# All turns of a two-layer decoder by DMA transposes, with every engine's order laid out by the kernel itself

## The chip, the cores and the metric

The kernel runs on one core of a Trainium2 chip. The core has a matrix engine (PE; PEld is its loading of weights), a vector engine (DVE), a scalar engine (ACT), a general engine (POOL) and an engine that issues transfers (SP); sixteen DMA engines carry the transfers. Each engine works through its own list of instructions in order and waits on semaphores for the others. The metric is the time of one execution on the device, in microseconds (us); lower is better.

## The reference

Two layers over 256 positions of width 1024. In each layer one input projection makes eight groups of 512 columns, two mixers of four heads each use them, an output projection adds to the residual stream, and a gated embedding is added after it:

```python
for i in range(DEPTH):                                 # DEPTH = 2
    h = rms_norm(x, norm_g[i])
    proj = h @ w_in[i]                                 # 1024 x 4096
    rq, rk, rv, rz, mq, mk, mv, mz = jnp.split(proj, cuts, axis=-1)
    r_out = retention(rotary(heads(rq)), rotary(heads(rk)), heads(rv), ret_norm_g[i])
    r_out = jax.nn.silu(rz) * r_out
    m_out = moba(rms_norm(heads(mq), q_norm_g[i]), rms_norm(heads(mk), k_norm_g[i]), heads(mv), rel_bias)
    m_out = jax.nn.silu(mz) * m_out
    x = x + jnp.concatenate([r_out, m_out], -1) @ w_out[i]
    gate = jax.nn.sigmoid(rms_norm(x) @ w_ple_gate[i])
    x = x + gate * rms_norm(p[i] @ w_ple[i], ple_norm_g[i])
```

At this length `moba` is plain causal softmax attention with a bias by distance, and `retention` is causal attention with a fixed decay in place of the softmax, followed by a norm per head.

## The kernel before

Every large product is made in three matmuls. Both factors are split into a high and a low part, and the kernel adds high by high, high by low and low by high (`mm3`, lines 143 to 148). I call these three matmuls a triple: they take one block of 128 inputs for one half `m` of the 256 positions to 512 outputs. A stage of weights (1 MB, `stage`, line 122) is loaded into one of four buffers `wst`, and `load_w` (lines 129 to 141) splits each half of it: ACT casts the high part `wh`, DVE subtracts it to get the low part `wl`. Six such pairs of parts exist. Each pair feeds 4 triples.

In a layer PE goes through the groups MQ, MK, RQ, RK, MZ, MV, RV, RZ (16 triples each), then the output projection (32 triples, `acc` banks filled first from the moba half, then from the retention half, line 612 and line 630), then the gate (32 triples, line 668). The attention matmuls are put in between: `moba_scores` (line 474), `moba_out` (510), `ret_scores` (525), `ret_out` (539).

What a matmul reads as its left factor has to lie with its inputs along the partitions, so results have to be turned. The kernel does it in two ways.

* By DMA: `halves` (line 252) lets ACT copy a 128x512 block of 4-byte values into two planes of 16-bit halves `u`; `turned_by_dma` (258) issues one DMA transpose of both planes into `w`, and two DVE copies put the halves together again (line 265). The heads of MQ, MK, RQ, RK and both mixers' outputs go this way: 12 blocks a layer.
* By PE: `transposed` (line 248) multiplies four 128x128 blocks with an identity (line 250) into a PSUM bank. ACT copies it out (line 497), or ACT and DVE split it into high and low parts (`evac_parts`, lines 283 and 284). The softmax probabilities (`turn`, 493: three blocks a layer) and the residual stream (`turn_x`, 625: four blocks of `x1T` in each layer, and four of the next layer's input `aT` after layer 0) go this way: 18 blocks of four matmuls.

The order on PE and SP is the order in which the code is written (`manual_schedule`, line 59): work behind a result is put off by a number of ticks (`later` and `tick`, lines 82 to 94), weight loads are called ahead when buffers come free. The instructions of ACT, DVE and POOL are laid by the framework's own scheduler, by priorities (`PRIO`).

Of the kernel before, what the change touches and what calls it, by code (L numbers as in the profile page):

```python
# [11 lines left out]
F32 = mybir.dt.float32  # L12
# [6 lines left out]
P = 128  # L19
# [18 lines left out]
PRIO = 300  # L38
AHEAD = 3
LATE = 5  # L40
# [12 lines left out]


@with_exitstack
def tile_hybrid_trunk(ctx: ExitStack, tc: tile.TileContext, first, rest, x, pT, ple_g, rel_bias,
                      w_in, w_out, w_ple, w_gate, consts, out):
    nc = tc.nc
    ctx.enter_context(tc.manual_schedule(engines={mybir.EngineType.PE, mybir.EngineType.SP}))
# [4 lines left out]

    cp = pool("cp", 1)
# [5 lines left out]
    big = pool("big", 2)  # L71
    tmp_p = pool("tmp", 4)
    tok_p = pool("tok", 3)
    sm = pool("sm", 4)
# [4 lines left out]
    pending = []  # L79
    now = [0]  # L80

    def later(delay, fn, prio=PRIO):

        pending.append((now[0] + delay, fn, prio))

    def tick():
        now[0] += 1
        tick_now()

    def tick_now():  # L90
        due = [e for e in pending if e[0] <= now[0]]
        pending[:] = [e for e in pending if e[0] > now[0]]
        for _, f, prio in due:
            with tc.high_priority(offset=prio):
                f()

    jobs, got = [], {}

    def job(key, fn):
        jobs.append((key, fn))  # L100

    def fetch(key):

        while key not in got:
            load_next()
        used.add(key)
        return got[key]

    def load_next():
        k, fn = jobs.pop(0)  # L110
        r = fn()
        if k is not None:
            got[k] = r

    def ahead():

        while jobs and len(got) - len(used) <= AHEAD:
            load_next()

    used = set()  # L120

    def stage(key, src):
        def fn():
            st = wst_p.tile([P, 4, GW], F32, name="wst")
            nc.sync.dma_start(st, src)
            return st
        job(key, fn)

    def load_w(key):

        st = fetch(key)
        parts = []
        for c in range(2):
            hi = wh_p.tile([P, 2, GW], F32R, name="wh")
            lo = wl_p.tile([P, 2, GW], F32R, name="wl")
            s = st[:, 2 * c:2 * c + 2]
            nc.scalar.copy(hi, s)  # L137
            nc.vector.tensor_tensor(lo, s, hi.bitcast(F32), op=ALU.subtract)  # L138
            parts.append((hi, lo))
        ahead()  # L140
        return parts

    def mm3(ps, a, k, w, kk, start, stop):
        ah, al = a
        wh, wl = w
        nc.tensor.matmul(ps, ah[:, k], wh[:, kk], start=start, stop=False)  # L146
        nc.tensor.matmul(ps, ah[:, k], wl[:, kk], start=False, stop=False)  # L147
        nc.tensor.matmul(ps, al[:, k], wh[:, kk], start=False, stop=stop)  # L148

    def act_tiles():  # L150
        both = act_p.tile([P, KT, 2, S], F32R, name="a")
        hi, lo = both[:, :, 0], both[:, :, 1]
        return [(hi[:, :, m * P:(m + 1) * P], lo[:, :, m * P:(m + 1) * P]) for m in range(MT)], hi, lo, both

    def rsqrt(dst, src, scale):
        n = src.shape[-1]
        t = sm.tile([P, 8], F32, name="rs_t")
        nc.vector.tensor_scalar(t[:, :n], src, scale, EPS, op0=ALU.mult, op1=ALU.add)  # L158
        nc.gpsimd.tensor_tensor(dst, t[:, :n], neghalf[:, :n], op=ALU.pow)  # L159

    par = cp.tile([P, Q_END], F32, name="par")
    warm = sm.tile([P, 1], F32, name="warm")
# [5 lines left out]
    for i in range(WARM):  # L168
        nc.tensor.matmul(ps0, idle[:, :P], idle, start=True, stop=True)
    x_t = xp.tile([P, MT, D], F32, name="x_t")  # L170
# [7 lines left out]
    bt = tmp_p.tile([P, GW], F32, name="tmp")[:H, :SPAN]  # L178
# [5 lines left out]
    def bias_table():  # L184
# [8 lines left out]
        d = dram.tile([H, SPAN], F32, name="bd")  # L193
        job(None, lambda: nc.sync.dma_start(d, bt))
        return bass.AP(tensor=d.tensor, offset=d.offset, ap=[[1, P], [SPAN, H], [1, S]])

    tbias = cp.tile([P, H, S], F32, name="tb")

    a0, a0h, a0l, a0b = act_tiles()

    def first_blocks(half):


        def fn():
            got = []
            for c in range(2):
                if half:
                    t = wst_p.tile([P, 4, GW], F32, name="wst").rearrange("p k n -> p (k n)")
                else:
                    t = xp.tile([P, MT, D], F32, name="E", bufs=2).rearrange("p m n -> p (m n)")  # L210
                at = 0
                for j in range(2):
                    k = half * 4 + 2 * c + j
# [551 lines left out]
```

## Time and profile before

| | us |
|---|---|
| median of 3 runs | 314.04 (314.0 to 314.89) |
| the profiled execution's own time | 314.63 |
| its span | 312.5 |
| PE busy | 307.1 (98%) |
| DVE busy | 241.4 (77%) |
| ACT busy | 190.6 (61%) |
| POOL busy | 27.4 (9%) |

The times of the parts below are read from the profiled execution. Its span begins with the first instruction and ends with the last; 2.1 us of its time lie around the span. A matmul's duration in the profile is longer than the distance to the next, since matmuls are pipelined; the distance is what counts for a sum.

### The profile page before, as it was taken

To read this page: it belongs to the slowest core of one execution; us is meant where nothing else is said; L and a number is where in the kernel's file an instruction comes from. 1 tells how busy PE (TensorE), PEld (TensorE's weight loads), DVE (VectorE), ACT (ScalarE), POOL (GpSimd) and SP (SyncE) were. 2 spreads that over 40 slices of the span, in tenths; PEclk is the share of its full clock that TensorE was granted. 3 is DMA by queue.
4 is the path that set the end of the run, shared out by engine and by line. 5 is a ranking of instruction groups with operands and counts; after the bars stand their busy time and mean duration, and the time that the engine had idled before them with its cause. 6 is when DMAs were issued, how large, how long until landed. Compare 5 with 4: busy or idle time off the path is not lost.

```text
span 312.5 us, 4188 instructions
## 1 busy us (share of the span) xinstructions
PE 307.1 (98%) x1465; PEld 255.8 (82%) x1465; DVE 241.4 (77%) x434; ACT 190.6 (61%) x330; POOL 27.4 (9%) x45
## 2 busy tenths in 40 slices
PE   8999999999999999999999999999999999999994
PEld 4888888888888888888888888888888888888884
DVE  4798899875599986949698877989747798959632
ACT  5887973866553746845485988447736536557411
POOL 4015100000002000101001521000000012000000
PEclk9999999999999999999999999999999999999998
DMA  7999949659791099200997569750496950770001
GB/s 266 419 412 415 273 90 401 115 122 382 274 348 55 6 262 421 87 0 24 379 397 271 198 127 297 303 160 0 115 367 258 289 181 2 176 294 2 34 35 67
DMA packets 35844, 65.03 MB, mean 208 GB/s; under 512 B 26476, under 2 KB 27248, under 8 KB 29680
## 3 DMA queue, kind: packets, MB, share of 16 engines
q1 hardware_dynamic: 35816, 64.78, 61.0%
q8 instruction: 11, 0.18, 0.2%
q14 instruction: 9, 0.07, 0.1%
q10 hardware_dynamic: 8, 0.00, 0.0%
HBM read 57.42 MB, written 1.05 MB: 187 GB/s over the span
## 4 chain that ended last, share of the span: by engine, by line
PE 97%; DMA 1%; DVE 1%; ACT 0%; issue 0%
PE acc L147 28%; PE acc L148 28%; PE acc L146 28%; PE mix L506 3%; PE mix L250 3%; PE mix L482 2%; PE mix L146 1%; PE mix L147 1%; PE mix L148 1%; DMA E<-in_first 1%; PE mix L528 1%; PE mix L529 1%; DVE wl L243 0%; DVE a L241 0%; ACT tmp L660 0%; DVE tmp L661 0%
## 5 line engine op out<-in xcount | busy, mean ns | idle before, releaser
L146 PE MATMUL acc<-wh,a 128*128 128x512 f32 (+1 forms) x392 | 153.3, 391 | 0.0
L147 PE MATMUL acc<-wl,a 128*128 128x512 f32 (+1 forms) x392 | 151.3, 386 | 0.1
L148 PE MATMUL acc<-wh,a 128*128 128x512 f32 (+1 forms) x392 | 151.2, 386 | 0.0
L137 ACT CAST wh<-wst 128x1024 fp32r<-128x1024 f32 x96 | 99.2, 1055 | 55.1 <-PE acc L148 33.7
L138 DVE TENSOR_TENSOR wl<-wst,wh 128x1024 fp32r<-128x1024 f32 x96 | 115.7, 1218 | 16.1 <-ACT wh L137 15.7
L146 PEld LDWEIGHTS acc<-wh,a 128*128 128x128 f32 x392 | 73.9, 189 | 14.7 <-ACT wh L236 0.6
L148 PEld LDWEIGHTS acc<-wh,a 128*128 128x128 f32 x392 | 73.8, 188 | 14.9
L147 PEld LDWEIGHTS acc<-wl,a 128*128 128x128 f32 x392 | 73.8, 188 | 14.7 <-DVE wl L243 0.6
L255 ACT COPY u<-tok 128x1024 uint16<-128x1024 uint16 x24 | 25.2, 1056 | 7.8 <-DVE tok L518 5.5
L265 DVE COPY T<-w 128x512 uint16<-128x512 uint16 x32 | 12.9, 454 | 8.9 <-DMA w<-u 8.9
L660 ACT ACTIVATE tmp<-acc,hr 128x512 f32<-128x512 f32 (+1 forms) x9 | 5.8, 640 | 19.4 <-PE acc L148 17.7
L159 POOL TENSOR_TENSOR ro<-rs_t,neghalf 128x4 f32<-128x4 f32 x4 | 4.9, 1234 | 134.9 <-DVE rs_t L158 134.9
L661 DVE SCALAR_TENSOR_TENSOR tmp<-tmp,E 128x512 f32<-128x512 f32 (+1 forms) x9 | 5.7, 631 | 13.7 <-ACT tmp L660 13.7
L283 ACT CAST a<-tmp 128x512 fp32r<-128x512 f32 x12 | 7.4, 618 | 10.4 <-DVE tmp L280 5.7
L506 PEld LDWEIGHTS mix<-V,PS 128*128 128x128 f32 x96 | 11.3, 192 | 0.3
L265 DVE COPY tmp<-w 128x512 uint16<-128x512 uint16 x16 | 6.4, 454 | 6.7 <-DMA w<-u 6.6
L506 PE MATMUL mix<-V,PS 128*128 128x128 f32 x96 | 11.4, 275 | 0.0
L434 POOL TENSOR_TENSOR qr<-qms,neghalf 128x4 f32<-128x4 f32 x8 | 10.0, 1263 | 13.5 <-DVE qms L432 10.5
L429 ACT ACTIVATE tmp<-acc 128x128 f32<-128x128 f32 x32 | 8.4, 289 | 1.4 <-PE acc L148 1.4
L284 DVE TENSOR_TENSOR a<-tmp,a 128x512 fp32r<-128x512 f32 x12 | 8.2, 682 | 0.7 <-ACT a L283 0.7
L283 ACT CAST a<-mix 128x512 fp32r<-128x512 f32 x8 | 4.7, 583 | 5.7 <-PE mix L250 5.6
L469 ACT ACTIVATE tmp<-acc,hr 128x512 f32<-128x512 f32 x8 | 5.5, 701 | 3.8 <-PE acc L148 3.8
(96 smaller groups left out, 255.9 us busy)
## 6 DMA issues: line engine op xcount, KB each, us to landing
wst<-in_w_in SPq DMA_DIRECT2D x30, 1024.0 KB, 7.6
wst<-in_w_out SPq DMA_DIRECT2D x8, 1024.0 KB, 5.0
wst<-in_w_gate SPq DMA_DIRECT2D x8, 1024.0 KB, 8.6
wst<-in_w_ple SPq DMA_DIRECT2D x2, 1024.0 KB, 6.0
wst<-in_rest SPq DMA_DIRECT2D x4, 384.0 KB, 6.6
E<-in_rest SPq DMA_DIRECT2D x3, 384.0 KB, 4.9
x_t<-in_x SPq DMA_DIRECT2D x2, 512.0 KB, 11.3
gb<-in_ple_g SPq DMA_DIRECT2D x2, 512.0 KB, 5.9
```

The costliest lines, as they stand in the source:

```text
L137: nc.scalar.copy(hi, s)
L138: nc.vector.tensor_tensor(lo, s, hi.bitcast(F32), op=ALU.subtract)
L146: nc.tensor.matmul(ps, ah[:, k], wh[:, kk], start=start, stop=False)
L147: nc.tensor.matmul(ps, ah[:, k], wl[:, kk], start=False, stop=False)
L148: nc.tensor.matmul(ps, al[:, k], wh[:, kk], start=False, stop=stop)
L250: nc.tensor.transpose(ps[:, j * P:(j + 1) * P], src[:, b * P:(b + 1) * P], ident)
L255: nc.scalar.copy(u, src.bitcast(U16).rearrange("p (n t) -> p t n", t=2))
L265: nc.vector.tensor_copy(raw[:, t], w[:, t])
L283: nc.scalar.copy(h, src)
L429: nc.scalar.activation(junk[:, sl], ps[m][:, sl], AF.Square, accum_out=ss[:, h:h + 1])
L434: nc.gpsimd.tensor_tensor(r, t, neghalf[:, :H], op=ALU.pow)
L506: nc.tensor.matmul(ps[:, h * DH:(h + 1) * DH], lhs(h, m, b), v[:, b, h * DH:(h + 1) * DH], start=b == 0, stop=b == m)
```

## The change

The identity and all 72 matmuls with it are gone. Probabilities and residual stream are turned as the heads already were: `halves` on ACT, one DMA transpose, two copies on DVE, and for the residual stream the split into high and low parts from the buffer in SBUF.

The ticks, the queue of load jobs and the priorities are replaced by a planner. `Flow` keeps a clock for each engine and one for the DMA engines. Each piece of work is a generator that names, step by step, its engine, an estimated duration and what it needs (`ask`); the planner takes the step that could start first, and among those that could start by then the one with the smallest key (a due time on PE's clock), and the step's instruction is written then. So the order of ACT, DVE, POOL and SP is fixed in the program too.

The order of PE changes in four places. Layer 0's moba scores stand after 58 triples instead of 64. Layer 1 projects MQ and MK together, by halves of the positions. `embed` (24 matmuls of the embedding) stands whole between the output projection and the gate in each layer, instead of in pieces around the gate. And the turns are gone.

The core of the diff:

```diff
-    ident = cp.tile([P, P], F32, name="ident")
-    make_identity(nc, ident)
...
-    ctx.enter_context(tc.manual_schedule(engines={mybir.EngineType.PE, mybir.EngineType.SP}))
+    ctx.enter_context(tc.manual_schedule(engines={E_.PE, E_.SP, E_.Activation, E_.DVE, E_.Pool}))
...
+class Flow:
...
+    def pick(self):
+        best = None
+        by = {}
+        for c in self.live:
+            r = self.can(c)
+            if r is not None:
+                by.setdefault(c.want[0], []).append((r, c))
+        for eng, cs in by.items():
+            start = max(self.clock[eng], min(r for r, _ in cs))
+            if best is None or start < best[0]:
+                best = start, eng, cs
+        if best is None:
+            return None
+        start, eng, cs = best
+        return start, min((c for r, c in cs if r <= start), key=lambda c: c.key() if callable(c.key) else c.key)
+
+    def lay(self, start, c):
+        eng, cost, take, after, mb = c.want
...
+        self.end = self.clock[eng] = start + cost
+        c.ready, c.on = self.end, eng
+        if mb is not None:
+            self.dma = max(self.dma, start + 1.3) + (2.7 * mb if mb else 0.8)
+            c.ready = self.dma + 0.9
...
-    def transposed(src, blocks, ps):
-        for j, b in enumerate(blocks):
-            nc.tensor.transpose(ps[:, j * P:(j + 1) * P], src[:, b * P:(b + 1) * P], ident)
-
-    def halves(src):
-
-        u = tok_p.tile([P, 2, GW], U16, name="u16", bufs=3)
+    def halves(src, name):
+
+        yield ask(ACT, 0.95, take=("u16",))
+        u = tok_p.tile([P, 2, GW], U16, name="u16", bufs=U_BUFS)
         nc.scalar.copy(u, src.bitcast(U16).rearrange("p (n t) -> p t n", t=2))
...
+    def turned(u, raw, take=()):
+
+
+        yield ask(SP, 1.25, take=("w16",), mb=TURN)
+        w = tok_p.tile([P, 2, 4, P], U16, name="w16", bufs=W_BUFS)
+        nc.sync.dma_start(w.rearrange("p t h k -> p (t h) k"), u.rearrange("p t n -> p (t n)"),
+                          transpose=True)
+        yield ask(DVE, 0.35, take=take)
...
+            nc.vector.tensor_copy(v, w[:, t].rearrange("p (h b) k -> p h (b k)", h=v.shape[1]))
...
-            def turn():
-
-                pt = mix_p.tile([P, 512], F32, name="mix")
-                transposed(s, range(4), pt)
-                nc.scalar.copy(PT[:, h0:h0 + per, m * P:m * P + n], pt.rearrange("p (h t) -> p h t", h=per))
-            later(7, turn)
...
+            u = yield from halves(s, "tok")
+            raw = box["PT"].bitcast(U16).rearrange("p h (k t) -> p t h k", t=2)
+            yield from turned(u, lambda: raw[:, :, h0:h0 + per, m * P:m * P + n])
...
-        def turn_x(dst, m, n, gains=None):
-            pt = mix_p.tile([P, 512], F32, name="mix")
-            transposed(x_t[:, m, n * GW:(n + 1) * GW], range(4), pt)
-            evac_parts(dst[m], n * 4, pt, 4, gains)
...
+        def added(m, n, ps):
+            xs = x_t[:, m, n * GW:(n + 1) * GW]
+            yield ask(DVE, 0.605)
+            nc.vector.tensor_tensor(xs, ps, xs, op=ALU.add)
+            flow.free("acc")
+            u = yield from halves(xs, None)
+            sq.append(flow.begin(squares([xs], SQ[m][:, n:n + 1]), flow.soon(3), flow.end))
+            yield from to_parts(x1T, m, n * 4, u)
...
+        groups.append(([both(TC, MQ, MK), lambda: [L_B]], moba_scores, 3, 2.5))
+        groups.append(([lambda: [PC.get(k) for k in ((0, 0), (1, 0), (1, 2))], both(VC, MV), both(TC, RQ, RK)],
+                       moba_out, 2, 2.0))
```

How the instructions stand at three places. First PE in layer 0, in the last triples of the output projection for the first half of the positions, before (L250 is the turn, `mix` its PSUM bank, `x_t` the residual stream):

```order
L146 MATMUL acc_1106<-wh_1214,a_140 128x512
L147 MATMUL acc_1106<-wl_1215,a_140 128x512
L148 MATMUL acc_1106<-wh_1214,a_140 128x512
L250 MATMUL mix_1247<-ident_115,x_t_111 128x128 x4
L146 MATMUL acc_1107<-wh_1200,a_140 128x512
L147 MATMUL acc_1107<-wl_1201,a_140 128x512
L148 MATMUL acc_1107<-wh_1200,a_140 128x512
```

And PE at the end of the same projection, now (L580 and L581 are the first of the 24 matmuls of `embed`):

```order
L314 MATMUL acc_1177<-wh_1171,a_125 128x512
L315 MATMUL acc_1177<-wl_1172,a_125 128x512
L316 MATMUL acc_1177<-wh_1171,a_125 128x512
L580 MATMUL mix_1299<-wh_1193,ph_392 128x512
L581 MATMUL mix_1299<-wl_1194,ph_392 128x512
```

No turn stands between the triples any more, and `embed` follows the projection directly.

Second, DVE at the same place, before (L639 adds the projection to the residual stream, L284 makes the low part of a turned block, L138 that of a weight tile):

```order
L639 TENSOR_TENSOR x_t_111<-acc_1105,x_t_111 128x512
L639 TENSOR_TENSOR x_t_111<-acc_1106,x_t_111 128x512
L284 TENSOR_TENSOR a_1197<-mix_1247,a_1197 128x4x128
L645 TENSOR_TENSOR ssq1_1294<-ssq_1198 128x1
L158 TENSOR_SCALAR rs_t_1297<-ssq1_1294 128x1
L649 TENSOR_SCALAR hr1_1300<-r1_1296 128x1
L138 TENSOR_TENSOR wl_1365<-wst_1208,wh_1364 128x1024
L639 TENSOR_TENSOR x_t_111<-acc_1107,x_t_111 128x512
```

And DVE there now (L902 is the addition, L469 the copies behind a DMA transpose, L488 the low part, L273 a weight tile):

```order
L902 TENSOR_TENSOR x_t_111<-acc_1117,x_t_111 128x512
L902 TENSOR_TENSOR x_t_111<-acc_1165,x_t_111 128x512
L469 COPY tmp_1275<-w16_1250 128x512 x2
L902 TENSOR_TENSOR x_t_111<-acc_1124,x_t_111 128x512
L273 TENSOR_TENSOR wl_1268<-wst_1089,wh_1267 128x1024
L488 TENSOR_TENSOR a_1209<-tmp_1275,a_1209 128x4x128
L469 COPY tmp_1307<-w16_1270 128x512 x2
L273 TENSOR_TENSOR wl_1288<-wst_1089,wh_1287 128x1024
L902 TENSOR_TENSOR x_t_111<-acc_1177,x_t_111 128x512
```

Each block has two copies more, and they stand in front of the next block's addition and the weight tiles.

Third, SP in layer 0 around the first head turns, before (`w16_430` and `w16_441` are MQ's, `w16_487` and `w16_497` MK's):

```order
L125 DMA wst_269<-in_w_in 128x2048
L125 DMA wst_357<-in_w_in 128x2048
L125 DMA wst_421<-in_w_in 128x2048
L262 DMA_TRANSPOSE w16_430<-u16_321 128x8x128
L262 DMA_TRANSPOSE w16_441<-u16_335 128x8x128
L125 DMA wst_466<-in_w_in 128x2048
L262 DMA_TRANSPOSE w16_487<-u16_395 128x8x128
L262 DMA_TRANSPOSE w16_497<-u16_409 128x8x128
```

And SP there now (`w16_418` and `w16_434` are MQ's, `w16_493` and `w16_504` MK's):

```order
L261 DMA wst_267<-in_w_in 128x2048
L437 DMA tb_118<-bd_123 128x4x256
L261 DMA wst_345<-in_w_in 128x2048
L460 DMA_TRANSPOSE w16_418<-u16_339 128x8x128
L460 DMA_TRANSPOSE w16_434<-u16_355 128x8x128
L261 DMA wst_447<-in_w_in 128x2048
L261 DMA wst_468<-in_w_in 128x2048
L460 DMA_TRANSPOSE w16_493<-u16_456 128x8x128
L460 DMA_TRANSPOSE w16_504<-u16_488 128x8x128
```

MK's turns stand behind two weight loads instead of one.

## Rows read from the trace of the kernel before

**Rows 1.** The head of the profile's page: the span, and each engine's busy time, share and instructions.

```profile
span 312.5 us, 4188 instructions
...
PE 307.1 (98%) x1465; PEld 255.8 (82%) x1465; DVE 241.4 (77%) x434; ACT 190.6 (61%) x330; POOL 27.4 (9%) x45
```

**Rows 2.** The chain that ended last, from the page: shares of the span by engine, tile and line.

```profile
PE acc L147 28%; PE acc L148 28%; PE acc L146 28%; PE mix L506 3%; PE mix L250 3%; PE mix L482 2%; PE mix L146 1%; PE mix L147 1%; PE mix L148 1%; DMA E<-in_first 1%; PE mix L528 1%; PE mix L529 1%; DVE wl L243 0%; DVE a L241 0%; ACT tmp L660 0%; DVE tmp L661 0%
```

**Rows 3.** Pieces of that chain in order of time: start, length, engine, tile and line. The turns in it are two pieces of 12 matmuls and twelve pieces of 4; one of the first kind and the first and last of the second are shown.

```profile
0.72 3.47 DMA E<-in_first
...
5.77 0.80 PE acc L147
...
49.75 2.62 PE mix L482 x16
...
61.91 1.31 PE mix L250 x12
...
121.61 0.44 PE mix L250 x4
...
289.92 0.44 PE mix L250 x4
...
308.42 0.48 ACT tmp L660
```

**Rows 4.** The timeline of PE about 27 us: start, duration, line and shapes. The two are nine matmuls apart.

```profile
25.79 0.39 PE L146 MATMUL acc<-wh,a 128*128 128x512 f32 x1
...
27.83 0.39 PE L146 MATMUL acc<-wh,a 128*128 128x512 f32 x1
```

**Rows 5.** Groups by line and form: engine, operation, shapes, count, then busy us and mean ns of one, then idle time before them.

```profile
L138 DVE TENSOR_TENSOR wl<-wst,wh 128x1024 fp32r<-128x1024 f32 x96 | 115.7, 1218 | 16.1 <-ACT wh L137 15.7
...
L255 ACT COPY u<-tok 128x1024 uint16<-128x1024 uint16 x24 | 25.2, 1056 | 7.8 <-DVE tok L518 5.5 <-DVE tok L455 1.3 <-DVE tok L562 0.6
...
L434 POOL TENSOR_TENSOR qr<-qms,neghalf 128x4 f32<-128x4 f32 x8 | 10.0, 1263 | 13.5 <-DVE qms L432 10.5 <-DVE rs_t L158 2.5 <-DVE rstd L387 0.5
L429 ACT ACTIVATE tmp<-acc 128x128 f32<-128x128 f32 x32 | 8.4, 289 | 1.4 <-PE acc L148 1.4
...
L283 ACT CAST a<-tmp 128x512 fp32r<-128x512 f32 x12 | 7.4, 618 | 10.4 <-DVE tmp L280 5.7 <-DVE tmp L265 4.7
L250 PE MATMUL mix<-ident,x_t 128*128 128x128 f32 x48 | 7.2, 272 | 0.0
...
L639 DVE TENSOR_TENSOR x_t<-acc,x_t 128x512 f32<-128x512 f32 x8 | 5.5, 687 | 2.6 <-PE acc L148 2.6
L284 DVE TENSOR_TENSOR a<-mix,a 128x512 fp32r<-128x512 f32 x8 | 5.5, 686 | 1.8 <-ACT a L283 1.8
...
L283 ACT CAST a<-mix 128x512 fp32r<-128x512 f32 x8 | 4.7, 583 | 5.7 <-PE mix L250 5.6
...
L497 ACT COPY PS<-mix 128x512 f32<-128x512 f32 x6 | 3.2, 594 | 1.0 <-PE mix L250 1.0
...
L250 PE MATMUL mix<-ident,tok 128*128 128x128 f32 x24 | 2.9, 273 | 0.0
```

**Rows 6.** The tile `w` of the DMA turns: the copies behind them and the transposes, with count and duration in ns (least, median, most; for SP that is the time to issue), then the time from issue to landing (us).

```profile
L265 DVE COPY T<-w x32: 442/450/473, 39.4 to 229.8; 128x512 uint16<-128x512 uint16 x32
L262 SPq DMA_TRANSPOSE w<-u x24: 1232/1244/5473, 28.9 to 268.2; - x24
L265 DVE COPY tmp<-w x16: 441/453/467, 86.1 to 271.9; 128x512 uint16<-128x512 uint16 x16
...
DMA to landing us min/median/max: 3.0/3.2/11.7
```

**Rows 7.** The timeline of DVE in layer 0: MK's copies (L265) ahead of the moba scores, then the window of the residual stream's turns. Start, duration, line; in brackets idle time and what ended it.

```profile
45.45 0.80 DVE L265 COPY T<-w 128x512 uint16<-128x512 uint16 x2
...
48.40 0.79 DVE L265 COPY T<-w 128x512 uint16<-128x512 uint16 x2
...
120.26 0.68 DVE L639 TENSOR_TENSOR x_t<-acc,x_t 128x512 f32<-128x512 f32 x1
121.65 0.69 DVE L639 TENSOR_TENSOR x_t<-acc,x_t 128x512 f32<-128x512 f32 x1 [0.70 <-PE acc L148]
...
133.25 1.41 DVE L325 SCALAR_TENSOR_TENSOR E<-mix,her,gb 128x512 f32<-128x512 f32 x2
```

**Rows 8.** The timeline of SP in layer 0: MK's two turns, and the three weight loads in front of the next turn. Start, length, line.

```profile
40.30 4.24 SPq L262 DMA_TRANSPOSE w<-u  x2
...
45.20 1.46 SPq L125 DMA_DIRECT2D wst<-in_w_in  x3
```

**Rows 9.** The timeline of ACT: the copies into halves for MK in layer 0. Start, duration, line.

```profile
33.14 1.10 ACT L255 COPY u<-tok 128x1024 uint16<-128x1024 uint16 x1
...
37.19 1.03 ACT L255 COPY u<-tok 128x1024 uint16<-128x1024 uint16 x1
```

**Rows 10.** Windows of 5 us: busy us of PE, PEld, DVE, ACT, POOL (instructions), PE's granted clock, DMA's share, GB/s.

```profile
25.00:30.00 5.00, 5.00 (x24) 4.14 (x23) 4.39 (x6) 3.62 (x16) 1.73 (x3) 1.00 1.03 424
...
45.00:50.00 5.00, 5.00 (x25) 4.18 (x25) 5.00 (x9) 2.35 (x3) 0.00 (x0) 1.00 1.00 307
50.00:55.00 5.00, 5.00 (x27) 4.31 (x27) 5.00 (x8) 2.00 (x2) 0.00 (x0) 1.00 1.02 410
...
265.00:270.00 5.00, 5.00 (x24) 4.14 (x23) 4.83 (x8) 3.50 (x5) 0.00 (x0) 1.00 0.42 80
```

More of the change, by code (lines that the diff above doesn't have):

```diff
@@ L52, with __init__, next @@
 Q_END = Q_KG + DEPTH
+PE, ACT, DVE, POOL, SP = range(5)
+ROW = 0.227
+TILE = 12 * ROW
+HOP = 0.15
+TURN = 0
+BACKLOG = 3.0
+U_BUFS, W_BUFS, T_BUFS = 3, 2, 3
+class Chain:
+    def __init__(self, gen, key, at):
+        self.gen, self.key, self.ready, self.done, self.on = gen, key, at, False, None
+        self.next()
+    def next(self):
+        try:
+            self.want = next(self.gen)
+        except StopIteration:
+            self.want, self.done = None, True
+class Mark:
+    done, ready = False, 0.0
@@ L55, in tile_hybrid_trunk, with ask @@
+def ask(eng, cost, take=(), after=(), mb=None):
+    return eng, cost, take, after, mb
 @with_exitstack
@@ L102, in fetch @@
[L102 to L159, printed above, removed]
+    def small(n, name):
+        return sm.tile([P, n], F32, name=name)
@@ new lines, in tile_hybrid_trunk, with tick, force_groups @@
+    groups = []
+    def tick():
+        while groups:
+            conds, fn, banks, margin = groups[0]
+            cs = [c for f in conds for c in f()]
+            if any(c is None for c in cs) or not all(c.done and c.ready + margin <= flow.clock[PE] for c in cs):
+                return
+            if sum(t <= flow.clock[PE] for t in flow.free_at["mix"]) < banks:
+                return
+            groups.pop(0)
+            fn()
+    def force_groups():
+        while groups:
+            conds, fn, *_ = groups.pop(0)
+            for f in conds:
+                for c in f():
+                    flow.need(c)
+            fn()
@@ new lines, in made, with rsqrt, squares @@
+    def made(a, m, k0, c):
+        for k in range(k0, k0 + 4):
+            a.made[m, k] = c
+        return c
+    def rsqrt(dst, src, scale, us):
+        n = src.shape[-1]
+        t = small(8, "rs_t")
+        yield ask(DVE, 0.1)
+        nc.vector.tensor_scalar(t[:, :n], src, scale, EPS, op0=ALU.mult, op1=ALU.add)
+        yield ask(POOL, us)
+        nc.gpsimd.tensor_tensor(dst, t[:, :n], neghalf[:, :n], op=ALU.pow)
+    def squares(srcs, t, bank=None):
+        for j, s in enumerate(srcs):
+            yield ask(ACT, 0.62, take=("tmp",))
@@ new lines, in tile_hybrid_trunk, with x_stats @@
+    E, ST_X = {}, {}
+    DONE = [[Mark() for _ in range(2)] for _ in range(MT)]
+    def x_stats(l, m, after=()):
+        if l:
+            t = small(2, "ssq")
+            yield ask(ACT, 0.0, after=after)
+            yield from squares([x_t[:, m, :GW], x_t[:, m, GW:]], t)
+            ss = yield from summed(t)
+        else:
+            yield ask(DVE, 1.15, take=("tmp",), after=after)
+            ss = small(1, "ssq1")
+            junk = tmp_p.tile([P, D], mybir.dt.bfloat16, name="tmp")
+            nc.vector.scalar_tensor_tensor(junk, x_t[:, m], 1.0, x_t[:, m], op0=ALU.mult,
+                                           op1=ALU.mult, accum_out=ss)
+            flow.free("tmp")
+        e = small(1, "epsx")
+        yield ask(DVE, 0.1)
+        nc.vector.tensor_scalar(e, ss, EPS / D, EPS * EPS, op0=ALU.mult, op1=ALU.add)
+        ST_X[l, m, "e"] = e
+        ST_X[l, m] = flow.begin(x_scale(l, m, ss), flow.soon(4 if l else 8), flow.end)
@@ new lines, in layer, with hr1 @@
+                    if m and k % 2:
+                        st.free(k // 2)
+                made(x1T, m, n * 4, flow.begin(added(m, n, acc[m][n]), flow.soon(0)))
+        embed(l)
+        def hr1(m, after):
+            yield ask(DVE, 0.0, after=after)
+            s = yield from summed(SQ[m])
+            r, h = small(1, "r1"), small(1, "hr1")
+            yield from rsqrt(r, s, 1.0 / D, 0.6)
+            yield ask(DVE, 0.1)
+            nc.vector.tensor_scalar(h, r, 0.5, None, op0=ALU.mult)
+            HR[m, "v"] = h
```

893 lines of the change are left out of this document (528 added, 365 removed).

## The prediction

> **What bounds the kernel now.** I read the page's head first: PE is busy 307.1 of 312.5 us, DVE 241.4, ACT 190.6 [rows 1]. That alone proves little, since pipelined matmuls look busy while they wait. So next the chain of waits: nearly all of it is PE, in triples and attention matmuls, and the turns (L250) hold 3% of it [rows 2]. In order of time the chain leaves PE only at the two ends: the first transfer and splits until 5.77, and the last tanh, two DVE operations and the store behind 308.42 [rows 3]. Then the pace: nine matmuls of 512 columns take 2.04 us, 0.227 each, so a triple takes 0.68 [rows 4]. In the 5-us windows PE shows no idle time, at a granted clock of 1.00, even where DVE is full for 10 us on end [rows 10]. So the time is PE's list, laid end to end, plus two ends. What leaves that list is gained one to one, as long as nobody keeps PE waiting. The whole forecast turns on the second half of that sentence.
>
> **What goes.** 72 matmuls with the identity: 48 for the residual stream and 24 for the probabilities [rows 5]. Their busy times there (7.2 and 2.9 us) overlap with their neighbours; the chain gives what they take from PE's time: twelve pieces of 0.44 us and two of 1.31 [rows 3], 5.3 + 2.6 = 7.9 us. ACT loses six copies out of PSUM of 0.594 us, 3.6 us; its eight casts of turned blocks read SBUF instead of PSUM, 0.618 for 0.583, 0.3 us more [rows 5]. None of ACT's is on the chain. The other matmuls stay the same in number and shape.
>
> **What comes.** 18 turns by DMA. Each has a copy into halves on ACT (1.06 us [rows 5]), an issue on SP (1.24), a flight (3.2 us from issue to landing at the median, 3.0 to 11.7) and two copies on DVE (0.45 each alone, 0.80 as a pair [rows 6, 7]). In sum ACT gets 19.0 us, SP 22.3 and DVE 14.4. ACT would stand at about 206 us and DVE at 256, against some 305: 68% and 84%. For the DMA engines, a window with one turn and most of another has a share of 0.42, or 2.1 us [rows 10]; I take 1.3 us a turn (bounds 1.0 and 2.1), 23 us for 18. All of this lies beside PE's list, and is free if each turn ends before PE needs its block. The cover must be counted at each place.
>
> *Residual stream, both layers.* Each block's first reader in the gate comes 20 triples after the block's last: for the first block 12 triples of the projection are left and the 24 matmuls of `embed`, 8 triples' worth, follow; for the last one `embed` and 12 triples of the gate. That is 20 x 0.68 = 13.6 us. The chain of one block: addition 0.69, halves 1.06, flight 3.2, copies 0.80, cast 0.62, low part 0.69 [rows 5 to 7], 7.1 us. Alone it has 6.5 us to spare. But the four blocks share DVE with weight tiles. In layer 0 the second addition waits for PE until 121.65 [rows 7]; without the 1.31 us of turns ahead of it that is 120.3, so the first block is ready at 117.6 and the last one is needed 32 triples later, at 139.4: 21.8 us. In the new order DVE has in that stretch 4 additions (2.8 us), 4 pairs of copies (3.2), 4 low parts (2.8), 5 weight tiles of 1.22 (6.1), a pair for E of 1.41 and nine small ones of some 0.15: 17.7 us. It also waits 2.0 us for the second block and 1.6 for the first landing: 21.3. Started back to back, operations follow each other some 0.08 us faster than their durations say, which is 2 us over 27 of them. So 0.5 to 2.5 us to spare: the tightest place. I take no stall.
>
> *The next layer's input.* Each block has 24 triples, 16.3 us, to its reader, for a chain of 9.2 us (tanh, two DVE operations and a multiplication by the gains stand in place of the addition; I put each at the addition's 0.69). To spare: 7 us alone; 3 to 4 when I walk DVE's list there. No stall.
>
> *Layer 0's scores* come six triples earlier, at 49.75 - 4.1 = 45.65 [rows 3]. Before, MK's copies ended at 49.2 [rows 7], but the transposes had been put off: their halves were ready at 34.2 and 38.2, and the first was issued at 40.30 [rows 8, 9]. Now they go when ready, behind two weight loads. The DMA engines are full there. Up to MK's turns some 13.9 MB are asked for: first blocks 3.2, eight stages 8.4, x, tables. At 424 GB/s [rows 10] from about 3 us that is 36, with MQ's two turns 38.6; MK's land at 41 to 42.5, and the copies behind the first rotary block of RQ end at about 43.5. To spare: 2 us.
>
> *Probabilities.* They land 44 triples (30 us) ahead of `moba_out`. Nothing.
>
> *MQ and MK together in layer 1.* RQ's second bank is MK's first one, free 9 triples (6.1 us) after its last matmul. Four squares with their sums, at most twice 0.29 each, POOL's power of 1.26 [rows 5], a product like the addition's 0.69 and a small operation make 3 to 4.5 us. To spare: 2.
>
> *The order laid by estimates.* ACT, DVE and SP now wait in written order, so a late transposed block holds up the weight tiles behind the copies, and those hold up PE. Weight tiles have, by the same walk, 2 to 6 us to spare. The estimates that set the order are 0.35 for a copy that takes 0.40 in a pair and 1.135 for a weight tile, where starts are 1.13 to 1.15 apart: close enough that lists hardly drift against PE. An engine that waits 1 us for another costs nothing while this holds. Bounds: nothing, to the 14.4 us that DVE gets, if all of it pushed PE. I take 0.4 us for handovers that I can't see, nearest to the windows in which DVE was full and PE lost nothing [rows 10]. Below nothing this term can't go, as PE had no idle time between the ends to win back.
>
> *The ends.* The first block still needs one transfer, an ACT cast and three DVE operations; the last chunk the same four steps. I take 0, bounds -0.5 and +0.5.
>
> **The sum.** 314.63 (profiled) - 7.9 + 0.4 = 307.1 on the profiled execution's own scale. The median lies 0.59 lower, which gives 306.5.
>
> A page speaks against the change. The Trainium skill, "VectorE: DVE Perf Modes", section "The three transpose paths", gives 390 ns for a 128x128 turn on TensorE and 1309 ns for one by DMA, and its rules say to use TensorE where PSUM will do as the destination, as it did here. Four turns on PE took 0.44 us of PE [rows 3], one DMA turn 3.2 us to land [rows 6]: the trace agrees that the DMA path is the slower one. By the rule the new paths end later at 18 places, and only the cover decides; that outcome is the third case below.
>
> **The other cases.**
>
> DVE becomes the bound in parts. For it: windows of its list were at 5.00 of 5.00 [rows 10], and the work there gets three more pairs of copies (2.4 us); the residual stream's window gets 3.2 us. Against it: PE lost nothing there. If spare time is at its low end, the excess is 2.4 - 2.0 = 0.4 at the scores and 3.2 - 2.5 = 0.7, up to 2, at the residual stream: some 1.5 us a layer, 3 in all: 309.5. Decided when DVE's list at the gate's start is over 0.5 us longer than counted.
>
> Slower: turns land late. Three weight loads issued within 1.5 us [rows 8] stood ahead of the turn that took the longest, 11.7 us [rows 6]. The place is the same start of the gate, where gate weights and the next layer's weights are on the same queue of SP. A landing of 11.7 instead of 3.2 us is 8.5 late; less 2 to spare, PE stands 6.5 us in each layer, 13 in all: 306.5 + 13 = 319.5. It decides from a landing of 5.2 us on, and the kernel is slower than before when the stalls pass 7.9. Against it: by my walk the gate's loads in layer 0 are released before 115 us, and the first of these turns is issued at 119.
>
> No gain at all: PE's matmuls go, but the supply of weights sets the end. For it: DVE's 96 weight tiles take 115.7 us and waited for ACT 15.7 [rows 5]. Against it: it would have shown as idle PE before. Then about 314.
>
> **Numbers.** The forecast 70%, with a range of its own from 305.3 to 308.5; DVE in parts 17%; late landings 8%; no gain 5%. The measurement tells some 0.3% from no change, here 0.9 us. The forecast and DVE's case are faster: 87%; no gain is the same, 5%; late landings are slower, 8%. The range leaves out the last two and the top of DVE's case: 305.2 to 311.0. Its low end is 306.1 without stalls, and 0.9 for the start and the spread of the runs.
>
> **What would show it.** Right: no line of turns on PE, 42 DMA transposes instead of 24, PE's idle time between the ends under 1 us, a span near 305. Wrong: gaps in PE before a matmul that reads the turned residual stream, the gate's first weight tile, or layer 0's scores, with DVE's copies or the landing of a transpose as releaser. If DVE's busy time comes out far above 256 us, the copies were mis-sized; if PE's first triple starts later than 5.8, the new order of the first blocks costs at the start.

## The result and the profile after

The changed kernel takes 310.2 us at the median (310.1 to 312.1), the kernel before, run beside it, 314.3: a ratio of 0.988, 95% interval 0.984 to 0.992. By the medians it is faster by 4.1 us (by the means, from which the ratio is made, by 3.7). 306.5 had been forecast, 7.8 us less: the sign is right, half the gain is missing. Here and below, ratios leave out single executions that lie more than 1.5% above the fastest of their kernel, while medians and spreads have all of them.

The page's head, the queue of SP and the chain, as in [rows 1, 2]; the profiled execution took 310.27 us in all:

```profile
span 308.5 us, 4105 instructions
...
PE 300.1 (97%) x1393; PEld 247.6 (80%) x1393; DVE 254.4 (82%) x470; ACT 204.3 (66%) x342; POOL 32.8 (11%) x43
...
q1 hardware_dynamic: 54824, 69.50, 74.8%
...
PE 69%; DVE 15%; DMA 11%; issue 2%; POOL 1%; ACT 1%; POOLq 0%; ACTq 0%; DVEq 0%
```

PE has lost its 72 matmuls, DVE and ACT have what was worked out. The chain is the news: it was nearly all PE, and now a quarter of it runs over DVE and DMA. In order of time three of its pieces are (start, length, engine, tile):

```profile
184.54 8.79 DMA w<-u
193.36 0.80 DVE T L469 x2
...
269.69 5.27 DMA w<-u
```

The first two lie ahead of layer 1's scores. SP's timeline shows what was issued ahead of that turn, DVE's how long it stood, PE's who waited in the end:

```profile
178.24 0.57 SPq L241 DMA_DIRECT2D pf<-in_pT  x1
178.87 0.43 SPq L241 DMA_DIRECT2D gb<-in_ple_g  x1
179.43 0.35 SPq L261 DMA_DIRECT2D wst<-in_w_in  x1
181.70 1.24 SPq L460 DMA_TRANSPOSE w<-u  x1
183.91 0.33 SPq L261 DMA_DIRECT2D wst<-in_w_in  x1
184.54 2.16 SPq L460 DMA_TRANSPOSE w<-u  x1
```

```profile
193.36 0.79 DVE L469 COPY T<-w 128x512 uint16<-128x512 uint16 x2 [2.41 <-DMA w<-u]
```

```profile
191.76 1.05 PE L751 MATMUL mix<-T 128*128 128x128 f32 x8
194.30 1.97 PE L751 MATMUL mix<-T 128*128 128x256 f32 x8 [1.49 <-DVE T L469]
```

The last of these turns is MK's second one (in this layer the order is MQ, MK for the first half of the positions, then MQ, MK for the second). It was issued 0.63 us behind a weight load, which itself came behind MQ's second turn and 1.75 MB of loads, and its copies start 8.82 us after the issue. The other place is the gate's start in layer 1, DVE's timeline:

```profile
269.65 0.69 DVE L902 TENSOR_TENSOR x_t<-acc,x_t 128x512 f32<-128x512 f32 x1 [1.06 <-PE acc L316]
274.99 0.80 DVE L469 COPY tmp<-w 128x512 uint16<-128x512 uint16 x2 [4.65 <-DMA w<-u]
275.68 0.67 DVE L902 TENSOR_TENSOR x_t<-acc,x_t 128x512 f32<-128x512 f32 x1
276.27 1.21 DVE L273 TENSOR_TENSOR wl<-wst,wh 128x1024 fp32r<-128x1024 f32 x1
```

DVE stands 4.65 us before copies whose turn hasn't landed, while the third addition and a weight tile stand behind them in its written list. From there it has no pause to 292 us, and PE waits twice at the gate, 0.3 us each time. A third short wait, 0.2 us, stands before a weight tile in layer 0, at 63 us. All waits of PE between 10 and 304 us:

```profile
PE mix L751 <- DVE T L469: 1.5, 1, 1.5
PE acc L315 <- DVE wl L273: 0.5, 2, 0.3
PE acc L316 <- DVE her L565: 0.3, 1, 0.3
```

In the kernel before, this view is empty. The waits add up to 2.3 us; with the pipeline's slower restart behind each (measured from start to start) they cost some 3.4: the last matmul starts at 303.57, it was 308.10 (the lines below, before and after), so 4.53 earlier where 7.9 us of matmuls are gone. Behind it the span is 0.5 us longer than before (4.9 for 4.4).

```profile
308.10 0.28 PE L148 MATMUL acc<-wh,a 128*128 128x256 f32 x1
```

```profile
303.57 0.28 PE L316 MATMUL acc<-wh,a 128*128 128x256 f32 x1
```

The tile `w` of the turns, as in [rows 6], first before and then after (the trace holds the landing of 31 of the 42 turns):

```profile
  DMA w<-u: 15.5, 10
```

```profile
  DMA w<-u: 18.0, 13
...
DMA to landing us min/median/max: 3.0/3.9/11.4
```

DVE stood before copies 13 times, 18.0 us in all; before it was 10 times, 15.5 us, and PE never waited for it.

### The profile page after: what moved, and what is told of

The parts are those of the page before. It is cut to its first block, busy times and chain, and to the rows that moved or that the text cites. A ratio compares the mean times of both kernels' runs of the same rounds, so it can differ in the third digit from the quotient of the medians.

```text
span 308.5 us, 4105 instructions
## 1 busy us (share of the span) xinstructions
PE 300.1 (97%) x1393; PEld 247.6 (80%) x1393; DVE 254.4 (82%) x470; ACT 204.3 (66%) x342; POOL 32.8 (11%) x43
## 3 DMA queue, kind: packets, MB, share of 16 engines
q1 hardware_dynamic: 54824, 69.50, 74.8%
## 4 chain that ended last, share of the span: by engine, by line
PE 69%; DVE 15%; DMA 11%; issue 2%; POOL 1%; ACT 1%; POOLq 0%; ACTq 0%; DVEq 0%
PE acc L315 21%; PE acc L316 21%; PE acc L314 21%; DMA w<-u 10%; DVE wl L273 5%; PE mix L762 3%; DVE tmp L469 2%; DVE E L569 1%; DVE a L488 1%; PE mix L813 1%; DMA a<-in_first 1%; DVE x_t L902 1%; DVE T L469 1%; PE mix L751 1%; DVE tok L668 1%
## 5 line engine op out<-in xcount | busy, mean ns | idle before, releaser
L273 DVE TENSOR_TENSOR wl<-wst,wh 128x1024 fp32r<-128x1024 f32 x96 | 114.8, 1219 | 8.5 <-ACT wh L271 8.4
L450 ACT COPY u<-tok 128x1024 uint16<-128x1024 uint16 x30 | 31.5, 1049 | 19.7 <-DVE tok L668 7.4
L469 DVE COPY tmp<-w 128x512 uint16<-128x512 uint16 x40 | 16.5, 457 | 10.5 <-DMA w<-u 10.5
L486 ACT CAST a<-tmp 128x512 fp32r<-128x512 f32 x20 | 12.4, 622 | 18.3 <-DVE tmp L469 9.5
L502 POOL TENSOR_TENSOR ro<-rs_t,neghalf 128x4 f32<-128x4 f32 x4 | 7.7, 1914 | 132.7 <-DVE rs_t L500 132.7
L469 DVE COPY T<-w 128x512 uint16<-128x512 uint16 x32 | 12.8, 457 | 7.0 <-DMA w<-u 6.7
L450 ACT COPY u<-x_t 128x1024 uint16<-128x1024 uint16 x12 | 12.5, 1045 | 5.8 <-DVE x_t L902 3.4
L488 DVE TENSOR_TENSOR a<-tmp,a 128x512 fp32r<-128x512 f32 x20 | 13.7, 684 | 0.0
L502 POOL TENSOR_TENSOR er<-rs_t,neghalf 128x1 f32<-128x1 f32 x4 | 4.9, 1230 | 67.3 <-DVE rs_t L500 63.2
L644 POOL TENSOR_TENSOR qr<-qms,neghalf 128x4 f32<-128x4 f32 x8 | 8.4, 1063 | 28.7 <-DVE qms L642 15.9
L733 ACT ACTIVATE tok<-tok,nm 128x128 f32<-128x128 f32 (+1 forms) x16 | 7.1, 447 | 5.4 <-DVE nm L730 5.4
```

The costliest lines, as they stand in the source:

```text
L450: nc.scalar.copy(u, src.bitcast(U16).rearrange("p (n t) -> p t n", t=2))
L469: nc.vector.tensor_copy(v, w[:, t].rearrange("p (h b) k -> p h (b k)", h=v.shape[1]))
L486: nc.scalar.copy(h, src)
L488: nc.vector.tensor_tensor(a.lo[:, k0:k0 + 4, m * P:(m + 1) * P], src, h.bitcast(F32), op=ALU.subtract)
L644: nc.gpsimd.tensor_tensor(r, t, neghalf[:, :H], op=ALU.pow)
```

## The experiments

Three theories. **Q**: turns land late because weight loads are issued just ahead of them on SP. **O**: DVE stands in its written order before copies, because the planner that wrote it didn't know the landings. **W**: the 14 us of copies given to DVE are simply too much. Every run stands against the kernel before, on the same chip.

| kernel | median us | ratio to before, interval |
|---|---|---|
| the change again | 311.3 | 0.990 (0.986 to 0.993) |
| turns first, both layers | 310.2 | 0.985 (0.982 to 0.988) |
| copies 2 us later | 308.8 | 0.982 (0.981 to 0.984) |
| all turns by DMA, old orders | 335.7 | 1.065 (1.062 to 1.068) |
| probabilities alone, old orders | 313.0 | 0.995 (0.993 to 0.996) |
| second copies on ACT | 322.9 | 1.027 (1.024 to 1.030) |
| 1.4 us more for mixed turns | 314.8 | 1.000 (0.998 to 1.002) |
| the same, loads standing back | 315.4 | 1.002 (0.999 to 1.005) |
| products for E put off | 311.0 | 0.988 (0.986 to 0.990) |
| later copies, E put off | 307.0 | 0.975 (0.973 to 0.977) |
| turns first in layer 1 | 308.1 | 0.980 (0.978 to 0.983) |
| PE's and SP's lists alone | 323.6 | 1.026 (1.023 to 1.029) |
| both edits | 306.5 | 0.975 (0.973 to 0.976) |

**The change again.** 

> The changed kernel once more, as the base for the runs beside it. Every theory: 310.2 us (309.9 to 310.6), a ratio to the kernel before of 0.988.

It came out at 309.5 to 314.5 us, a spread of more than 1%, while before stayed within 313.9 to 315.0. In its profiled execution (310.4 us) PE waited 0.9 us before layer 1's scores instead of 1.5. That the longer executions are longer by such waits is likely, but no trace of one is there to show it.

**Turns first.**

```diff
+        if mb and self.coming and self.dma >= 30 and (c.key() if callable(c.key) else c.key) > self.clock[PE] - LATEST:
+            return None
         return r if mb is None or self.dma < 30 else max(r, self.dma - BACKLOG)
...
+        flow.coming += 1
         yield ask(ACT, 0.95, take=("u16",))
...
+        flow.coming -= 1
         yield ask(DVE, 0.35, take=take)
```

> The changed kernel, but a load of weights that is not needed within 8 us stands back on SP from the moment a block's halves are due until its turn is issued. Theory Q (turns land late because a load of weights was issued just ahead of them): MK's second turn in layer 1 lands in under 5 us instead of 8.79, the 1.65 us gap of PE before the second matmul of the scores goes, the gap at the gate stays (its load is issued before the halves are due): 308.5 us, at most 309. Theory W (DVE's added copies, not the landings, make it late): MK's copies end as late as before since DVE is what is full, no more than 0.4 us gained: 309.8 to 310.6. Theory O (the order written by estimates): the order changes little, 309.8 to 310.4.

The wait before the scores fell to 0.2 us, yet the time hardly moved and spread from 308.1 to 313.9. The profiled execution is the longest of the six. It has a new wait in layer 0 (PE's timeline, then windows of PE: busy, granted clock, DMA share, GB/s):

```profile
66.95 0.69 PE L319 MATMUL acc<-wl,a 128*128 128x512 f32 x1 [2.53 <-DVE wl L277]
67.44 0.63 PE L320 MATMUL acc<-wh,a 128*128 128x512 f32 x1
67.87 0.63 PE L318 MATMUL acc<-wh,a 128*128 128x512 f32 x1
```

```profile
67.00:71.00 4.00, 4.00 (x11) 0.57 1.00 225
71.00:75.00 4.00, 4.00 (x19) 1.00 1.00 416
```

The loads held back were not what was missing there: between 50 and 66 us no engine waited for a load. The low part that PE waits for stood on DVE behind the copies of the probability turns, and these waited for their landings (6.67 us after the issue for the first turn, 7.95 for the second, each behind a weight load). Its cast had long been made on ACT (ACT's timeline, then DVE's; the tile is the 21st in both lists):

```profile
52.64 1.05 ACT L275 CAST wh<-wst 128x1024 fp32r<-128x1024 f32 x1
```

```profile
64.14 1.65 DVE L475 COPY PS<-w 128x512 uint16<-128x512 uint16 x4 [0.86 <-DMA w<-u]
65.68 3.48 DVE L277 TENSOR_TENSOR wl<-wst,wh 128x1024 fp32r<-128x1024 f32 x3
```

That is theory O's mechanism, now in layer 0. So in this execution the edit paid at one place and cost at another; whether the shorter ones had the wait, no trace shows. To judge Q it had to be kept to layer 1.

**Turns first in layer 1**, the same with `self.clock[PE] > 165.0` in place of `self.dma >= 30`.

> The changed kernel, but in layer 1 alone (from 165 us of the planner's clock on) loads of weights not needed within 8 us stand back while a block's halves are due, until its turn is issued. Layer 0's lists are those of the changed kernel. Theory Q: MK's second turn lands in 6 us or less instead of 8.79, the gap at the scores falls from 1.1 to 1.65 us to 0.4, 308.8 us (308.4 to 309.4). Theory O: the landing is what it is, within 0.5 us of 310.2.

308.1 us: Q holds. On SP MQ's second turn and MK's second turn now go together ahead of the load (first fence). MQ's lands 6.0 us after its issue; MK's, issued at 185.02, is read from 190.03 on without a wait, so at most 5.0 us after it. The 16 matmuls of the scores run in one piece (second fence), though they stand six matmuls earlier in PE's list than in the change:

```profile
182.18 4.36 SPq L465 DMA_TRANSPOSE w<-u  x2
186.64 1.00 SPq L265 DMA_DIRECT2D wst<-in_w_in  x2
```

```profile
191.06 2.78 PE L757 MATMUL mix<-T 128*128 128x128 f32 x16
```

The gaps at the gate went too: the turn there was issued at 267.71, its copies started 4.9 us later, and DVE stood 3.34 us instead of 4.65.

**Copies 2 us later** in the planner's list.

```diff
-            c.ready = self.dma + 0.9
+            c.ready = self.dma + (0.9 if mb else 2.9)
```

> The changed kernel, but the planner counts a turn as landing 2 us later than before, so that the copies stand further down in DVE's written list. Theory O (DVE stands idle in written order before copies whose turn hasn't landed, with ready work behind them): the idle 4.65 us of DVE before the first copies of the residual stream in layer 1 shrinks below 2.5 us, the two gaps of 0.59 us at the gate of layer 1 go, the gap at the scores stays or moves: 309.0 us (308.6 to 309.5). Theory Q: landings are where they were, 310.2 us within 0.4. Theory W: the sum of DVE's work is the same, 310.2 us within 0.4.

308.8 us: O holds as well. DVE stood 3.6 us in all before copies, not 18.0. At the gate of layer 1 one wait of 0.3 us was left of two, and the scores lost theirs, there since the planner had also moved them on PE (to 195.88 us, 12 matmuls later in its list). Landings were no better (median 4.6). New gaps came at the next layer's input, where copies 2 us later are too late, some 2 us.

**Products for E put off.**

```diff
-            ST_X[l, m, "E"] = flow.begin(scaled(m, ps), flow.soon(-5))
+            ST_X[l, m, "E"] = flow.begin(scaled(m, ps), flow.soon(8))
```

> The changed kernel, but the planner puts the products for E and their small operations behind what the gate's start needs (a start time 13 us later in its order of preference); landings and SP's order as they were. Theory C (from the landing on, DVE has no spare time before the gate's start in layer 1: 4.65 us stood idle, then work back to back, so what is put off there is gained): both gaps of 0.59 us in layer 1 go, 309.0 us (308.6 to 309.4), the gap at the scores stays. Theory Q (only the landing decides): gaps stay, within 0.4 us of 310.2.

A miss: 311.0. The two gaps went, and two of 0.95 us came at 295.2 and 297.7 before weight tiles, and one of 0.6 at 177.6. That stretch of DVE is full; what is moved in it costs elsewhere. The scores lost their gap here too, by chance: the new lists issued MK's second turn ahead of the load.

**Later copies except for the next layer's input, and E put off.**

```diff
-            c.ready = self.dma + 0.9
+            c.ready = self.dma + 0.9 - mb * (mb < 0)
...
-        yield ask(SP, 1.25, take=("w16",), mb=TURN)
+        yield ask(SP, 1.25, take=("w16",), mb=-late)
...
-                yield from to_parts(aN, m, n * 4, u, par[:, g0:g0 + 4])
+                yield from to_parts(aN, m, n * 4, u, par[:, g0:g0 + 4], late=0.0)
```

> The copies put 2 us later in the planner for all turns except those of the next layer's input, and the products for E put off as in the run beside it. Theories O and C: against the kernel with all copies 2 us later (308.8), the 1.9 us of gaps between 150 and 162 us and the 0.5 at the gate go: 306.4 us (306.0 to 307.2), which is what was forecast for the change. Theory Q: loads still stand ahead of turns, 308.5 us or more.

307.0 us, with no wait of PE over 0.2 us behind the first 11. MK's second turn still lands 7.3 us after its issue behind a load: a late landing cost nothing where the lists, PE's among them, counted on it.

**Both edits.** 

> The two edits together: copies counted as landing 2 us later except for the next layer's input, E put off, and in layer 1 loads of weights standing back for turns. Theory A (the two edits cure the same gaps by two ways): 306.9 us, within 0.6 of the first edit alone (306.98). Theory B (landings and the order in DVE are separate losses, each of which costs PE): the landing's edit adds some 1 us or more, 306.0 us or less.

306.5 us, 0.4 below the first edit alone, with intervals that overlap: one loss and two cures, as theory A had it. The profiled executions say it more sharply. From the 31st matmul, where the start is over, to the last one they take 297.3 us before, 292.8 in the change, and 289.3 with turns first in layer 1, 289.1 with later copies and E put off, 289.1 with both. What is left between the times of these three lies in the first 12 us and behind the last matmul. DVE's work is what it was, and it stands 3.2 us before copies. W falls with this (the page's head, the tile `w`, and PE's last matmul).

```profile
PE 299.0 (98%) x1393; PEld 247.9 (81%) x1393; DVE 255.1 (84%) x470; ACT 203.8 (67%) x342; POOL 31.5 (10%) x43
```

```profile
  DMA w<-u: 3.2, 5
...
DMA to landing us min/median/max: 3.0/3.6/10.0
```

```profile
300.17 0.28 PE L321 MATMUL acc<-wh,a 128*128 128x256 f32 x1
```

**Second copies on ACT** (of the turns into the gate).

```diff
-            nc.vector.tensor_copy(v, w[:, t].rearrange("p (h b) k -> p h (b k)", h=v.shape[1]))
+            s = w[:, t].rearrange("p (h b) k -> p h (b k)", h=v.shape[1])
+            if t and on == ACT:
+                nc.scalar.copy(v, s)
+            else:
+                nc.vector.tensor_copy(v, s)
```

> The changed kernel, but of each turn of the residual stream into the gate the second copy goes to ACT: 1.6 us less on DVE per layer. Theory W (DVE's added copies make the gate's parts late): both gaps of 0.59 us at the gate of layer 1 and the one of 0.33 in layer 0 go, 308.8 to 309.4 us. Theory O (DVE stands in written order before a turn that hasn't landed): DVE still stands 3 to 5 us before the first copy in layer 1, and the time moves by less than 0.5 us from 310.2.

Neither: 322.9 us. DVE's work fell by 1.2 us only (253.2 for 254.4), and ACT's casts of weights now stand in written order behind copies and squares; PE waited 5.4 us for low parts of weights and 3.8 for casts. This doesn't speak for or against W, as it loads ACT at the same place.

**1.4 us more for turns issued while a load is under way**, alone and with loads standing back.

```diff
+            mixed = 0.0 if mb or not self.loading or self.dma <= start + 1.3 else MIXED
+            self.loading = bool(mb)
-            self.dma = max(self.dma, start + 1.3) + (2.7 * mb if mb else 0.8)
+            self.dma = max(self.dma, start + 1.3) + (2.7 * mb if mb else 0.8 + mixed)
```

> The changed kernel, but the planner counts 1.4 us more for a turn that is issued while a load of weights is under way, as the trace shows it (turns land 3.05 us after issue alone, 5.3 to 8.8 behind loads); a turn alone counts as before. Theories O and Q: DVE's list now has ready work where it stood idle, PE's idle time between 20 and 300 us falls below 2 us from some 4, 308.0 us (307.3 to 308.8), not slower than the copies put 2 us later everywhere. Theory W: within 0.5 us of 310.2.

> The same planner with the 1.4 us, and loads of weights not needed within 14 us stand back while a block's halves are due, until its turn is issued. Theory Q (the issue order on SP is what costs): 0.5 us or more below the kernel without the standing back, 307.5 us. Theory O (what counts is that the lists know the landings): the same as without it within 0.4 us. Theory W: within 0.5 us of 310.2.

Both missed, by 7 and 8 us. DVE hardly stood before copies any more (4.9 and 1.7 us), but the new lists put both products for E ahead of the tile that the gate reads next (DVE, then PE; the releaser's name is that of the neighbouring operation, the tile ends at 287.30; the execution shown is the fastest of twelve, 311.6 us):

```profile
284.77 1.41 DVE L573 SCALAR_TENSOR_TENSOR E<-mix,her,gb 128x512 f32<-128x512 f32 x2
286.09 1.21 DVE L277 TENSOR_TENSOR wl<-wst,wh 128x1024 fp32r<-128x1024 f32 x1
```

```profile
287.36 0.50 PE L319 MATMUL acc<-wl,a 128*128 128x512 f32 x1 [2.93 <-DVE hr L930]
```

Better estimates of the landings are not enough by themselves: the planner picks by urgency as it guesses it and doesn't weigh a wait of PE. With loads standing back the like came in both layers (waits of 3.0 and 2.6 us). No run has these 1.4 us with both products put off; with the plain 2 us and the products put off, as above, PE doesn't wait there.

**All turns by DMA under the orders of before**: `halves` and two copies in place of the identity matmuls, ACT, DVE and POOL ordered by the framework.

```diff
-            pt = mix_p.tile([P, 512], F32, name="mix")
-            transposed(x_t[:, m, n * GW:(n + 1) * GW], range(4), pt)
-            evac_parts(dst[m], n * 4, pt, 4, gains)
+            with tc.high_priority(offset=PRIO):
+                parts_by_dma(dst[m], n * 4, halves(x_t[:, m, n * GW:(n + 1) * GW]), gains)
```

> The kernel before with all 18 turns by DMA, the instructions of ACT, DVE and POOL left in the order that the framework gives them, SP's in the order of the code: the change without its hand-laid lists. Theory Q: SP's order puts loads ahead of the turns here too, with landings of 6 us and more, and no planner that shifts PE's list: 312 us or more. Theory W: the work on DVE is the same as in the changed kernel, so the time is too: 310 us within 1. Theory O: free of the written order of DVE it does better than the changed kernel: 307 to 309 us.

335.7 us: the turns without the planner are far slower than no change, though landings are good (median 3.2) and the work the same. DVE stands 38.7 us before copies, and PE (windows as above) runs at less than its clock behind long waits:

```profile
150.00:180.00 30.00, 20.04 (x65) 0.77 0.87 257
```

**Probabilities alone**, the same edit at `turn` in `moba_scores`, one tick behind the scores.

> The kernel before with the probabilities alone turned by DMA (6 turns; 24 matmuls with the identity gone), the residual stream still by PE, orders as before. Theory P (a turn whose block is needed 30 us later is free in any order): 314.4 - 2.6 = 311.8 us, at most 312.3. Theory O (the orders of before don't bear more turns, wherever they stand): 314 us or more, with new waits of PE.

Between the two: 313.0. The last matmul starts 1.67 us earlier; one new wait of 0.7 (a low part at 116 us) takes the rest of the 2.6.

**PE's and SP's lists alone.**

```diff
-    ctx.enter_context(tc.manual_schedule(engines={E_.PE, E_.SP, E_.Activation, E_.DVE, E_.Pool}))
+    ctx.enter_context(tc.manual_schedule(engines={E_.PE, E_.SP}))
```

> The changed kernel with PE's and SP's lists as they are, instruction for instruction, but ACT, DVE and POOL in the order that the framework gives them. Theory O in its strong form (the hand-laid lists of ACT and DVE are what carries the change, as 335.7 us under the old orders suggested): 320 us or more. Theory S (the 335.7 came from SP's order and PE's list, which the planner shifts; the lists of ACT and DVE matter little): 308 to 312 us, with DVE's idle time before the copies in layer 1 other than 4.65 us.

323.6 us: O in its strong form. With PE's and SP's lists unchanged, DVE in the framework's order stood 37.2 us before copies, and PE waited (10 to 320 us):

```profile
PE acc L316 <- DVE a L488: 5.9, 5, 3.6
PE mix L751 <- DVE T L469: 3.6, 2, 2.9
PE acc L314 <- ACT a L486: 2.3, 1, 2.3
```

Roughly, and taken in this order, of the 25 us between 335.7 and 310.2, 12 lie in PE's and SP's lists and 13 in those of the others; the two slow kernels also run at a lower mean clock of PE (0.97 and 0.985).

## Why the prediction was half right

- **What goes**: right. In the kernel with both edits, where PE waits for nobody, the last matmul starts at 300.17, 7.93 us earlier than before; 7.9 was the sum. Counted from the 31st matmul on it is 8.2, so the agreement to 0.03 is luck; the size is not.
- **What comes**: DVE 256 forecast, 254.4 measured; ACT 206 and 204.3; 42 transposes. DMA was somewhat too low: the queue's share rose from 61.0% of 312.5 us to 74.8% of 308.5, 40 us for 18 turns, 2.2 each, where I took 1.3 with a bound of 2.1. But 10 of the 40 us are the loads' packets of 8 KB, which took longer (130.2 us of all sixteen engines before, 139.9 after); the turns' own packets of 256 bytes took 36.7 us for 24 turns and 66.9 for 42, 1.6 a turn.
- **Layer 0's scores**: PE doesn't wait, as forecast, but with less to spare. MK's second turn landed at 43.44 and its copies ended at 44.27, where at most 42.5 and about 43.5 were worked out; the scores start at 45.41, so 1.1 us were to spare, not 2. **Probabilities and the next layer's input**: no wait over 0.1 us, right here; the run with later copies shows how little is to spare at the latter.
- **Residual stream, "I take no stall"**: failed. The flight went in at its median of 3.2; in layer 0 it was 4.15 and in layer 1 5.27. The rival had its threshold right (a landing of 5.2 us) and its reason against wrong: the last gate load isn't released before 115 us but at 118.60, 2.3 us ahead of the first turn (120.88), and in layer 1 at 267.41, again 2.3 us ahead. PE's two gaps there cost 1.2 us, one in layer 0 0.3.
- **MQ and MK together in layer 1**: failed by leaving out. I counted the handover of a bank and not the scores, which read the same turns; 1.65 us, the largest gap. With its copies at most 5.0 us behind the issue, as with turns first in layer 1, PE didn't wait.
- **The order laid by estimates, 0.4 us**: this is the term that was mis-sized, at some 3.4. I compared durations on DVE, which hold, and not landings, which don't: "an engine that waits 1 us for another costs nothing" is no longer true where DVE is full behind the wait. The bounds (to 14.4) held it.
- **The ends**: the start as before (the 31st matmul at 10.73 for 10.83; over the profiled executions it varies from 10.3 to 12.0); the end 0.5 longer, at the bound. The last store is issued 1.73 us behind the last matmul in both, so the 0.5 lies behind that issue; why is not explained.
- **The rivals**: "late landings" had 8% and 13 us; it was its mechanism at a quarter of that price, at one of its two places and at the scores. "DVE becomes the bound" gave nearly the time (309.5), but 255.1 us of DVE in 306.5, with no wait of PE, shows it wrong as a cause. What remains of it: a full DVE passes each delay on.
- The Trainium skill's figures for the two paths ("VectorE: DVE Perf Modes", "The three transpose paths") compare one bf16 transpose with one. Here the path that is slower by itself won, as it lies beside PE. What it needed to win was the order: the same 18 turns gave 306.5 and 335.7 us.

## What to carry to other kernels

In this kernel, work moved from the bounding engine to a queue was gained in full only where the landings and the lists of the engines behind them agreed. So look up, for each transfer, what is issued ahead of it on its queue, and what stands behind its consumer on an engine that runs in written order. Take the flight at that place, not the median. Where a planner lays the lists, check its estimates of landings first, and try each change of them, since one delay cured moves the next.

## What was not expected

- **The clock.** Behind a wait of 2.5 to 2.7 us PE's granted clock can fall to 0.50, which is 1.2 GHz: in the run with copies on ACT it had five matmuls in 5 us, between waits of 1.02 and 2.67, and the next ones started 0.43 us apart instead of 0.227 (windows, then the timeline). A wait of 2.93 us in the profile with the 1.4 us did not do this. Among that kernel's twelve times 311.6 us goes with a mean clock of 1.00 and 316.1 with 0.986: a gap of this length may cost much more in one execution than in the next, though no trace of the slower ones shows it.

```profile
134.00:139.00 5.00, 1.41 (x5) 0.98 0.68 67
139.00:142.00 3.00, 2.90 (x6) 0.50 0.00 0
```

```profile
140.55 0.63 PE L315 MATMUL acc<-wl,a 128*128 128x512 f32 x1
140.98 0.63 PE L316 MATMUL acc<-wh,a 128*128 128x512 f32 x1
```

- **A turn is dear on the DMA engines**: 1.6 us of all sixteen by its own packets, 2.2 if all that the queue's share rose by is put down to it, though it lands 3.0 us after its issue when alone. The Trainium skill ("DMA: Bandwidth & Descriptors", "Queues, rings and completion order") says that descriptors of one ring are taken up in order; the landings behind loads agree, 8.8 us for MK's second turn with a load 0.63 us ahead and at most 5.0 for the same turn ahead of that load.
